# Queueing the scan's inverse blocks and the SSM's inputs behind the inverses' last stores

## The chip, the cores and the metric

The kernel runs on one core of one Trainium2 chip. A core has five engines that run side by side, each through its own list of instructions in a fixed order: TensorE (PE, with its weight loads shown as PEld), VectorE (DVE), ScalarE (ACT), GpSimd (POOL) and SyncE (SP). SP does no arithmetic here; it issues transfers (DMAs), one after the other. An instruction that waits for a semaphore holds up everything behind it on the same engine. A DMA is an issue on a queue (about half a microsecond of SP's time in this trace) and then the moving of the bytes by 16 shared DMA engines; its end is seen by others through a semaphore.

The metric is the device time of one launch in microseconds (us). Before the change it is 1614.11 us, the median of three runs (1608.63 to 1615.89).

## What is computed

One layer of a streaming encoder for 1024 prompt tokens and 32 sample tokens, 1056 columns in all. The layer is `x = LN(alpha*x + Mix(x))`, then `x = LN(alpha*x + MLP(x))`. Mix takes one input projection of x and feeds three groups: attention with a compressed KV latent (6 heads), an S5 state space model (the SSM, 16 groups with a 64-dimensional complex state) and RWKV-7 time mixing (6 heads of 64). Their outputs are joined and go through one output projection. The part of the reference around the change is the RWKV recurrence and the SSM's input:

```
def step(S, inp):                                   # RWKV, for each token
    r_t, w_t, k_t, v_t, kk_t, a_t = inp
    sa = einsum('bhij,bhj->bhi', S, -kk_t)
    S = S * w_t + sa[..., None] * (kk_t * a_t) + v_t[..., None] * k_t
    return S, einsum('bhij,bhj->bhi', S, r_t)

bu = einsum('gpc,btgc->btgp', b_bar, u_blk)         # SSM: inputs into states,
                                                    # then a scan over time and a readout
```

## The kernel before, in words

Stages. The input projection and all that is worked out per token for RWKV, attention and the SSM come first, up to about 300 us of the span. Then attention, RWKV and the SSM run interleaved, up to about 700 us. The output projection with the first layer norm follows, and from about 800 us on the MLP, where TensorE is almost always busy.

RWKV in chunks. The recurrence is done in chunks of 64 tokens as a triangular system. For each of the three pairs of heads (index p) and each chunk, a 64 x 64 unit-triangular matrix has to be inverted. `rwkv_inv` does it in two steps. First the 32 x 32 diagonal blocks are inverted on VectorE (31 steps on a tile `y`), and stored to DRAM: `zt_d` (transposed) and the fields 0 and 1 of `xt_d` (lines 765 and 766). Then they are loaded back in another layout as `zb` and `zc` (lines 777 and 778), and the off-diagonal block of each inverse is made by two rounds of small TensorE products (line 788), each followed by copies by VectorE out of PSUM (line 791). The second round's result, for p = 0, 1, 2, is stored to field 2 of `xt_d` at line 794: two DMAs for each p, six in all. The first four read `zb`, the last two `zc`. They are called the last stores below, S0, S1 and S2 by p.

The scan. `stage_rwkv` begins behind the inverses. It loads the two first blocks of operands `ld` (line 814), clears three tiles `xt` (POOL, line 1011), and fills them from `xt_d`: for each p six DMAs, four from the fields 0 and 1 (the diagonal blocks, lines 1015 and 1016) and two from field 2 (the off-diagonal block, line 1017), 18 in all. `xt` is read first in `rwkv_solve` (line 882). Ahead of that stands `rwkv_pairs`, which writes the tile `r` by DVE (line 835), ACT (line 841) and POOL (lines 853, 854). `r` and the SSM's tile `em` lie in memory that the inverses' tiles held before, so they wait for whatever read these tiles last: the last stores.

The SSM. `stage_s5` works in four quarters. Each loads `ut` from `u_d` (lines 619, 620), `em` (line 622), `ut`'s second part from `kt_d` by eight small DMAs (line 624) and `ces` from `tab_d` (line 628), multiplies `em` with `ut` on TensorE (line 633), loads `cl` over `em` (line 641), and goes on.

What sets the order. The kernel is written as generators: `stage_mix` yields the steps of attention with, from the 50th step on, a step of the SSM at every seventh; `stage_streams` yields the steps of the inverses and of the scan. `side_by_side` takes the steps of both in a fixed ratio. A planner at build time then orders each engine's instructions by dependencies, by its own estimate of the times and by priority: the order in which instructions were written, with the steps of `stage_streams` moved up by 120 places (`high_priority(PRIO)`). `issue_after(ins)` limits it: whatever is written inside the block on the engine of `ins` comes behind `ins` in that engine's list. It adds no semaphore. `side_by_side` uses it to keep TensorE's steps in the written order, and to hold SP's instructions of the second stream behind `g.sp_mark`, the last DMA of the first step of that stream (the load of `zc`, line 778). The SSM's steps are held behind `g.sp_mark` on SP too, and behind `g.scan_dve` on DVE. Where between the `zc` load and their consumers the 18 loads of `xt` and the SSM's loads stand in SP's list is left to the planner.

Of the kernel before, what the change touches and what calls it, by code (L numbers as in the profile page):

```python
# [406 lines left out]
def bc(ap, shape):  # L407
    return ap.broadcast_to(shape)
# [304 lines left out]
def hsl(i):  # L713
    return slice(64 * i, 64 * i + 64)
# [28 lines left out]
def rwkv_inv(g):  # L743


    nc = g.nc
    V = nc.vector
    H = 3 * NU
    nn = g.ip.tile([H, 2, 32, 32], F32, tag="nn", name="nn", bufs=1)
    yf = g.ip.tile([H, 2, 1024], F32, tag="y", name="y", bufs=1)  # L750
    y = yf.rearrange("v f (a b) -> v f a b", b=32)
    nc.gpsimd.memset(yf, 0.0)
    nc.gpsimd.memset(yf[:, :, 0:1024:33], 1.0)
    for p in range(3):
        (nc.sync if p % 2 else nc.scalar).dma_start(out=nn[NU * p:NU * p + NU], in_=g.mt_d[:, NU * p:NU * p + NU].rearrange("f v a b -> v f a b"))
    for s in range(31):
        m, n = s + 1, 31 - s
        tmp = g.ip.tile([H, 512], F32, tag="tmp", name="tmp", bufs=1)
        tv = tmp[:, :2 * m * n].rearrange("p (f m n) -> p f m n", f=2, n=n)
        V.tensor_tensor(out=tv, in0=bc(y[:, :, 0:m, s:s + 1], [H, 2, m, n]), in1=bc(nn[:, :, s:s + 1, s + 1:32], [H, 2, m, n]), op=ALU.mult)  # L760
        V.tensor_tensor(out=y[:, :, 0:m, s + 1:32], in0=y[:, :, 0:m, s + 1:32], in1=tv, op=ALU.add)
    yield
    zt = g.ip.tile([H, 32, 32], F32, tag="nn", name="zt", bufs=1)
    nc.scalar.activation(out=zt, in_=y[:, 0].rearrange("u i a -> u a i"), func=AF.Copy)
    nc.sync.dma_start(out=g.zt_d, in_=zt)
    nc.sync.dma_start(out=g.xt_d[:, 0:2], in_=y)

    zb = g.ip.tile([P, 2, 2, 16, 32], F32, tag="nn", name="zb", bufs=1)
    zc = g.ip.tile([P, 2, 16, 32], F32, tag="y", name="zc", bufs=1)
    parts = []  # L770
    for p in range(3):
        z, b = (zb[:, p, 0], zb[:, p, 1]) if p < 2 else (zc[:, 0], zc[:, 1])
        us = slice(NU * p, NU * p + NU)
        zs = g.zt_d[us].rearrange("(t c) a i -> c a t i", c=2)
        ys = g.xt_d[us].rearrange("(t c) f i j -> c f i t j", c=2)
        for c in range(2):
            nc.sync.dma_start(out=z[64 * c:64 * c + 32], in_=zs[c][:, 0:16])
            nc.sync.dma_start(out=z[64 * c + 32:64 * c + 64], in_=ys[c][1][:, 0:16])
        parts.append((z, b, ys))
    yield  # L780
    for o in (0, 32):
        for p, (z, b, ys) in enumerate(parts):
            l = b if o else g.n12[p]
            ps = g.pfs.tile([P, 16, 32], F32, tag="fs", name="pti")
            for t in range(16):
                for c in range(2):
                    rows = slice(64 * c + o, 64 * c + o + 32)
                    nc.tensor.matmul(out=ps[64 * c:64 * c + 32, t], lhsT=l[rows, t], rhs=z[rows, t], start=True, stop=True)
            for c in range(2):
                d = 64 * c + 32 - o  # L790
                V.tensor_copy(out=b[d:d + 32], in_=ps[64 * c:64 * c + 32])
            if o:
                for c in range(2):
                    nc.sync.dma_start(out=ys[c][2][:, 0:16], in_=b[64 * c:64 * c + 32])
            yield


# [8 lines left out]
def rwkv_load(g, t):  # L806

    nc = g.nc
    s, n = blk_tokens(t)
    ld = g.rp.tile([P, 3, 5, P], F32, tag="ld", name="ld", bufs=3)  # L810
    if n < P:
        nc.gpsimd.memset(ld, 0.0)
    for p in range(3):
        nc.sync.dma_start(out=ld[:, p, :, :n], in_=g.rw_d[p][:, 0:5, s:s + n])
    g.ld[t] = ld
# [45 lines left out]
def rwkv_nv(g, t):  # L861
    nc = g.nc
    r = g.r[t]
    pn = g.pr.tile([P, 3, 2, 64], F32, tag="pr", name="prn")
    for p in range(3):
        for h in range(2):
            for c in range(2):
                nc.tensor.matmul(out=pn[hsl(c), p, h], lhsT=r[hsl(c), p, K_N, h], rhs=r[hsl(c), p, K_V, h], start=True, stop=True)
    nc.scalar.activation(out=r[:, :, K_NV], in_=pn, func=AF.Copy)
# [106 lines left out]
def rwkv_norm(g, t):  # L976

    nc = g.nc
    s, n = blk_tokens(t)
    yc, sq = g.yc.pop(t)  # L980
    gate = g.rl.tile([P, 3, P], F32, tag="bg", name="gate", bufs=1)[:, :, :n]
    for p in range(3):
        nc.sync.dma_start(out=gate[:, p], in_=g.rw_d[p][:, 5, s:s + n])
    pv = g.pr.tile([P, 3, P], F32, tag="pr", name="prv")[:, :, :n]
    nc.tensor.matmul(out=pv, lhsT=g.bones, rhs=sq, start=True, stop=True)
    m = g.rl.tile([P, 3, P], F32, tag="m", name="m", bufs=1)[:, :, :n]
    nc.vector.tensor_scalar(out=m, in0=pv, scalar1=1.0 / 64, scalar2=GN_EPS, op0=ALU.mult, op1=ALU.add)
    iv = g.rl.tile([P, 3, P], F32, tag="iv", name="iv", bufs=1)[:, :, :n]
    rsqrt_newton(g, m, iv, sq)
    nc.vector.tensor_tensor(out=yc, in0=yc, in1=iv, op=ALU.mult)  # L990
    for p in range(3):
        nc.vector.tensor_scalar(out=yc[:, p], in0=yc[:, p], scalar1=g.vec[:, V_GNG + p:V_GNG + p + 1], scalar2=g.vec[:, V_GNB + p:V_GNB + p + 1], op0=ALU.mult, op1=ALU.add)
    nc.gpsimd.tensor_tensor(out=yc, in0=yc, in1=g.bn.pop(t), op=ALU.add)
    nc.gpsimd.tensor_tensor(out=yc, in0=yc, in1=gate, op=ALU.mult)
    s = TP if s == SOFF else s
    store(g, nc.gpsimd if t == ORDER[8] else None, g.mg_d[5:8, :, s:s + n].rearrange("k p t -> p k t"), yc)


def stage_rwkv(g):
    nc = g.nc  # L1000
    g.ld, g.r, g.wu, g.gq, g.xt, g.yb, g.yc, g.bn = {}, {}, {}, {}, {}, {}, {}, {}
    xts = [g.rp.tile([P, 9, 2, 64], F32, tag="xt", name="xt", bufs=3) for p in range(3)]
    for tag, n in (("wu", 1024), ("ut", NY * L5)):
        g.rp.tile([P, n], F32, tag=tag, name=tag, bufs=1)
    g.i2 = g.rp.tile([P, 64], F32, tag="i2", name="i2", bufs=1)
    nc.sync.dma_start(out=g.i2, in_=g.a["i2"])
    for t in ORDER[:2]:
        rwkv_load(g, t)
    for p in range(3):
        xt = xts[p]  # L1010
        nc.gpsimd.memset(xt, 0.0)
        src = g.xt_d[NU * p:NU * p + NU].rearrange("(t c) f i j -> c f i t j", c=2)
        for c in range(2):
            x = xt[hsl(c)].rearrange("p t h x -> p (t h) x")
            nc.sync.dma_start(out=x[0:32, :, 0:32], in_=src[c][0])
            nc.sync.dma_start(out=x[32:64, :, 32:64], in_=src[c][1])
            nc.sync.dma_start(out=x[0:32, 0:16, 32:64], in_=src[c][2][:, 0:16])
        g.xt[p] = xt

    for i in range(10):  # L1020
        t, u, v = (ORDER[j] if 0 <= j < 9 else None for j in (i, i - 1, i - 2))
        if i + 2 < 9:
            rwkv_load(g, ORDER[i + 2])
        if t is not None:
            yield from rwkv_pairs(g, t)
        if v is not None:
            rwkv_norm(g, v)
            yield
        if u is not None:
            g.yb[u] = g.rl.tile([P, 3, P], F32, tag="yb", name="yb", bufs=2)  # L1030
            yield from rwkv_ops(g, u)
        if t is not None:
            rwkv_nv(g, t)
            yield
            if u is not None:
                yield from rwkv_chain(g, u)
                rwkv_mean(g, u)
            rwkv_solve(g, t)
            yield
        if i == 8:  # L1040
            out_weights(g, WOUT[:3])
    out_weights(g, WOUT[3:])
# [251 lines left out]
def last_traced(g, engine):  # L1294

    return next(i for i in reversed(g.nc.cur_bb.bb.instructions) if i.engine == engine)
# [88 lines left out]
def out_weights(g, parts):  # L1385

    for k in parts:
        raw, hi, lo = g.wout_mem(k)
        load3(g, g.a["w_out"][:, k], raw, hi, lo)
        g.wout[k] = hi, lo  # L1390
# [118 lines left out]
def stage_mix(g):  # L1509

    with g.tc.tile_pool(name="pav", bufs=1, space=PSUM, reuse_waits="tile") as g.pav:
        ssm, n = stage_s5(g), 0
        for _ in stage_attn(g):
            yield
            n += 1
            if n > S5_FROM and n % S5_STEP == 0:
                with g.tc.issue_after(g.scan_dve), g.tc.issue_after(g.sp_mark):
                    next(ssm, None)
        for _ in ssm:
            yield  # L1520
# [354 lines left out]
```

## Time and profile before

| what | value |
|---|---|
| runs | 1614.11 us median (1608.63 to 1615.89) |
| profiled execution, its own time | 1613.95 us |
| its span, first to last instruction | 1612.2 us |
| mean granted TensorE clock | 0.964 |
| PE / PEld busy | 1488.8 / 1337.5 us (92% / 83%) |
| DVE / ACT / POOL busy | 920.5 / 510.7 / 416.5 us |
| DMA traffic | 123.50 MB in 112621 packets |

The times in the trace are microseconds from the span's first instruction. The rows of a timeline give the start, the duration, the engine, the line, the operation, the tiles and the count; the bracket behind a row gives how long the engine had been idle and which instruction or transfer ended the wait. Rows of SP are DMA issues, not the transfers themselves. In a table by stretches each engine has its busy time and, in brackets, its instructions, then the granted TensorE clock (1.00 is full), the mean busy share of the 16 DMA engines and GB/s.

### The profile page before, as it was taken

To read this page: it belongs to the slowest core of one execution; us is meant where nothing else is said; L and a number is where in the kernel's file an instruction comes from. 1 tells how busy PE (TensorE), PEld (TensorE's weight loads), DVE (VectorE), ACT (ScalarE), POOL (GpSimd) and SP (SyncE) were. 2 spreads that over 40 slices of the span, in tenths; PEclk is the share of its full clock that TensorE was granted. 3 is DMA by queue.
4 is the path that set the end of the run, shared out by engine and by line. 5 is a ranking of instruction groups with operands and counts; after the bars stand their busy time and mean duration, and the time that the engine had idled before them with its cause. 6 is when DMAs were issued, how large, how long until landed. Compare 5 with 4: busy or idle time off the path is not lost. (4 is left out here: it accounts for less than half of the span.)

```text
span 1612.2 us, 26346 instructions
## 1 busy us (share of the span) xinstructions
PE 1488.8 (92%) x10855; PEld 1337.5 (83%) x10855; DVE 920.5 (57%) x1676; ACT 510.7 (32%) x991; POOL 416.5 (26%) x394
## 2 busy tenths in 40 slices
PE   7899899587899888898999999999999999999995
PEld 7889786465667566566779999999999999999995
DVE  8466959363666544453865745454555454545458
ACT  4344433313544545542323111222111122221122
POOL 3713663520121101221412111222121112222123
PEclk9999999788999999999999999999999999999998
DMA  5314471372333221222612111111111111111012
GB/s 183 130 60 175 147 189 33 94 176 46 85 79 90 64 72 42 69 85 86 197 50 76 49 40 40 53 53 40 52 40 44 48 40 53 53 40 53 14 40 82
DMA packets 112621, 123.50 MB, mean 77 GB/s; under 512 B 51280, under 2 KB 87812, under 8 KB 112120
## 3 DMA queue, kind: packets, MB, share of 16 engines
q1 hardware_dynamic: 92516, 102.53, 21.9%
q10 hardware_dynamic: 19632, 18.27, 3.7%
q8 instruction: 85, 1.39, 0.4%
q0 software_dynamic: 352, 1.01, 0.2%
q14 instruction: 36, 0.29, 0.1%
HBM read 89.05 MB, written 32.68 MB: 76 GB/s over the span
## 5 line engine op out<-in xcount | busy, mean ns | idle before, releaser
L63 PE MATMUL acc<-xh,uphi 128*128 128x384 f32 (+1 forms) x768 | 248.9, 324 | 0.0
L65 PE MATMUL acc<-xl,uphi 128*128 128x384 f32 (+1 forms) x768 | 247.9, 323 | 0.0
L67 PE MATMUL acc<-xh,uplo 128*128 128x384 f32 (+1 forms) x768 | 247.6, 322 | 0.0
L1540 DVE TENSOR_TENSOR rl<-rl 128x384 f32<-128x384 f32 (+1 forms) x96 | 142.2, 1481 | 176.9 <-ACT rl L1539 175.3
L1568 DVE TENSOR_TENSOR yacc<-yacc,acc 128x384 f32<-128x384 f32 (+2 forms) x344 | 158.8, 507 | 111.7 <-PE acc L67 111.6
L63 PE MATMUL acc<-hh,dnhi 128*128 128x384 f32 (+2 forms) x736 | 209.2, 320 | 0.0
L65 PE MATMUL acc<-hl,dnhi 128*128 128x384 f32 (+2 forms) x736 | 207.1, 319 | 0.0
L67 PE MATMUL acc<-hh,dnlo 128*128 128x384 f32 (+2 forms) x736 | 197.4, 319 | 0.0
L50 POOL TENSOR_TENSOR dnlo<-dnraw,dnhi 128x1024 fp32r<-128x1024 f32 x30 | 72.5, 2418 | 337.7 <-ACT dnhi L49 322.4
L63 PEld LDWEIGHTS acc<-xh,uphi 128*128 128x128 f32 x768 | 144.1, 188 | 0.3 <-ACT xh L49 0.3
L65 PEld LDWEIGHTS acc<-xl,uphi 128*128 128x128 f32 x768 | 144.2, 188 | 0.0
L67 PEld LDWEIGHTS acc<-xh,uplo 128*128 128x128 f32 x768 | 144.2, 188 | 0.0
L50 POOL TENSOR_TENSOR uplo<-upraw,uphi 128x1024 fp32r<-128x1024 f32 x34 | 81.6, 2399 | 237.7 <-ACT uphi L49 237.7
L63 PE MATMUL acc<-xh,wmhi 128*128 128x384 f32 (+3 forms) x384 | 132.6, 345 | 9.3 <-ACT xh L49 8.4
L65 PE MATMUL acc<-xl,wmhi 128*128 128x384 f32 (+3 forms) x384 | 131.1, 341 | 1.6 <-DVE xl L50 1.6
L63 PEld LDWEIGHTS acc<-hh,dnhi 128*128 128x128 f32 x736 | 131.5, 188 | 0.0
L65 PEld LDWEIGHTS acc<-hl,dnhi 128*128 128x128 f32 x736 | 131.4, 188 | 0.0
L67 PE MATMUL acc<-xh,wmlo 128*128 128x384 f32 (+3 forms) x384 | 130.0, 339 | 0.0
L67 PEld LDWEIGHTS acc<-hh,dnlo 128*128 128x128 f32 x736 | 128.9, 188 | 0.0
L49 ACT ACTIVATE dnhi<-dnraw 128x1024 fp32r<-128x1024 f32 x30 | 31.8, 1060 | 299.8 <-PE acc L65 249.0
L1255 PE MATMUL av<-ptk,vo 128*128 128x512 f32 (+5 forms) x204 | 75.4, 453 | 22.3 <-POOL ptk L1282 19.2
L49 ACT ACTIVATE hh<-rl 128x384 fp32r<-128x384 f32 (+1 forms) x96 | 47.9, 499 | 148.9 <-DVE rl L1540 148.9
(489 smaller groups left out, 2880.5 us busy)
## 6 DMA issues: line engine op xcount, KB each, us to landing
upraw<-in_w_up SPq DMA_DIRECT2D x32, 512.0 KB
dnraw<-in_w_dn SPq DMA_DIRECT2D x30, 512.0 KB
ld<-rw SPq DMA_DIRECT2D x24, 320.0 KB
wmraw<-in_w_m SPq DMA_DIRECT2D x12, 512.0 KB
wo<-in_w_out SPq DMA_DIRECT2D x8, 512.0 KB
z<-in_xa SPq DMA_DIRECT2D x8, 512.0 KB
out_y<-o SPq DMA_DIRECT2D x8, 512.0 KB
xr<-in_xt SPq DMA_DIRECT2D x8, 384.0 KB
```

Source lines behind the costliest of these rows:

```text
L49: nc.scalar.activation(out=hi, in_=ps, func=AF.Copy)
L50: (lo_eng or nc.vector).tensor_tensor(out=lo, in0=ps, in1=hi.bitcast(F32), op=ALU.subtract)
L63: nc.tensor.matmul(out=outs[i], lhsT=lh, rhs=rhs[i][0], start=start, stop=False)
L65: nc.tensor.matmul(out=outs[i], lhsT=lh, rhs=rhs[i][1], start=False, stop=False)
L67: nc.tensor.matmul(out=outs[i], lhsT=ll, rhs=rhs[i][0], start=False, stop=stop)
L1255: nc.tensor.matmul(out=po[:, c:n], lhsT=vo[:w, kt].rearrange("p a x -> p (a x)")[:, 64 * i:64 * i + P], rhs=pt[:w, c:n], start=kt == tiles ...
L1540: nc.vector.tensor_tensor(out=r[:, :n], in0=r[:, :n], in1=r[:, :n], op=ALU.mult)
L1568: nc.vector.tensor_tensor(out=y, in0=y, in1=ps[i][:, :n], op=ALU.add)
```

## The change

Two limits on SP's list are changed. `rwkv_inv` now notes, after the last stores of each p, the last DMA written on SP as `g.inv_sp`; after p = 2 this is the second DMA of S2. The 18 loads of `xt` are written inside `issue_after(g.inv_sp)`, and the SSM's steps are held behind `g.inv_sp` instead of `g.sp_mark` on SP. No instruction is added or removed, no tile changes its size or place.

```
@@ rwkv_inv
             if o:
                 for c in range(2):
                     nc.sync.dma_start(out=ys[c][2][:, 0:16], in_=b[64 * c:64 * c + 32])
+                g.inv_sp = last_traced(g, mybir.EngineType.SP)
             yield
@@ stage_rwkv
-        for c in range(2):
-            x = xt[hsl(c)].rearrange("p t h x -> p (t h) x")
-            nc.sync.dma_start(out=x[0:32, :, 0:32], in_=src[c][0])
-            nc.sync.dma_start(out=x[32:64, :, 32:64], in_=src[c][1])
-            nc.sync.dma_start(out=x[0:32, 0:16, 32:64], in_=src[c][2][:, 0:16])
+        with g.tc.issue_after(g.inv_sp):
+            for c in range(2):
+                x = xt[hsl(c)].rearrange("p t h x -> p (t h) x")
+                nc.sync.dma_start(out=x[0:32, :, 0:32], in_=src[c][0])
+                nc.sync.dma_start(out=x[32:64, :, 32:64], in_=src[c][1])
+                nc.sync.dma_start(out=x[0:32, 0:16, 32:64], in_=src[c][2][:, 0:16])
         g.xt[p] = xt
@@ stage_mix
-                with g.tc.issue_after(g.scan_dve), g.tc.issue_after(g.sp_mark):
+                with g.tc.issue_after(g.scan_dve), g.tc.issue_after(g.inv_sp):
                     next(ssm, None)
```

## Prediction

> **What bounds the kernel now.** I read the busy shares of the page first, then a table by stretches, then the waits, and last the timelines of the engines around the inverses' last stores.
>
> ```profile
> PE 1488.8 (92%) x10855; PEld 1337.5 (83%) x10855; DVE 920.5 (57%) x1676; ACT 510.7 (32%) x991; POOL 416.5 (26%) x394
> ...
> 364.00:374.00 10.00, 0.12 (x2) 0.00 (x0) 2.30 (x5) 1.27 (x3) 2.87 (x5) 0.65 0.52 93
> 374.00:400.00 26.00, 25.73 (x247) 19.59 (x247) 10.65 (x28) 12.23 (x30) 0.65 (x5) 0.94 0.04 11
> 400.00:760.00 360.00, 322.31 (x3261) 239.61 (x3260) 189.67 (x413) 169.61 (x349) 54.26 (x111) 0.96 0.27 74
> ```
>
> TensorE (PE, first engine column) bounds the kernel as a whole. In the stretch from 364 to 374 us it does 0.12 us of work, while no other engine is busy for more than 2.87 us. Before and behind that hole it is close to full. The waits between 360 and 376 us name the cause:
>
> ```profile
> DVE r L835 <- DMA xt_d<-zc: 11.4, 1, 11.4
> POOL r L853 <- DMA xt_d<-zc: 10.7, 1, 10.7
> PE av L1255 <- POOL ptk L1282: 10.5, 2, 10.1
> ACT r L841 <- DMA xt_d<-zc: 7.7, 1, 7.7
> ```
>
> Three engines stop at the same transfer, the store of `zc` (S2), because `r` lies where `zc` lay. TensorE stops at `av`, which waits for a POOL memset that stands behind POOL's work on `r`. So the question is why S2 lands when it does. Here are VectorE's copies that make the data of the last stores, and then SP's list:
>
> ```profile
> 350.22 1.40 DVE L791 COPY zb<-pti 32x512 f32<-32x512 f32 x2 [1.25 <-PE pti L788]
> 355.75 1.40 DVE L791 COPY zb<-pti 32x512 f32<-32x512 f32 x2 [4.14 <-PE pti L788]
> ...
> 358.11 1.40 DVE L791 COPY zc<-pti 32x512 f32<-32x512 f32 x2 [0.23 <-PE pti L788]
> ```
>
> ```profile
> 338.59 0.52 SPq L619 DMA_DIRECT2D ut<-u_d x1
> 339.16 0.83 SPq L620 DMA_DIRECT2D ut<-u_d x1
> 340.03 0.84 SPq L628 DMA_DIRECT2D ces<-tab_d x1
> ...
> 347.61 1.68 SPq L814 DMA_DIRECT2D ld<-rw x3
> 349.39 0.46 SPq L1015 DMA_DIRECT2D xt<-xt_d x1
> ...
> 356.38 0.50 SPq L1016 DMA_DIRECT2D xt<-xt_d x1
> 356.97 3.97 SPq L624 DMA_DIRECT2D ut<-kt_d x5
> 361.04 1.07 SPq L794 DMA_DIRECT2D xt_d<-zb x2
> 362.16 0.54 SPq L624 DMA_DIRECT2D ut<-kt_d x1
> 363.08 0.86 SPq L1017 DMA_DIRECT2D xt<-xt_d x2
> 363.99 1.18 SPq L624 DMA_DIRECT2D ut<-kt_d x2
> 365.27 1.06 SPq L794 DMA_DIRECT2D xt_d<-zb x2
> 367.28 0.83 SPq L1017 DMA_DIRECT2D xt<-xt_d x2
> 368.22 0.96 SPq L794 DMA_DIRECT2D xt_d<-zc x2
> 370.28 0.84 SPq L1017 DMA_DIRECT2D xt<-xt_d x2
> 371.17 0.48 SPq L622 DMA_DIRECT2D em<-em_d x1
> ```
>
> The data of S0, S1 and S2 are ready at 351.62, 357.15 and 359.51 us (start plus duration of the copies). The stores go out at 361.04, 365.27 and 368.22: 9.4, 8.1 and 8.7 us later. In between SP is not waiting for data; it is issuing twelve loads of `xt` (349.39 to 356.88) and eight of `kt_d`, and between the stores it stands at line 1017 until the store before has landed. The queue, not the data, is what S2 waits for.
>
> **The change part by part.** No instruction is added; the edges carry no semaphore. Moved on SP are 16 of the 18 `xt` loads (only p = 2's two at line 1017 stood behind S2), `ut` x2, `ces` and the eight of `kt_d`. `em` stood behind S2 already. POOL's and ACT's queues carry none of them.
>
> *The stores.* SP gets to S0 no later than 349.29 (347.61 + 1.68) and then waits in turn for 351.62, 357.15 and 359.51. Whatever stands behind them on SP waits along, but that is now only the moved loads, `em`, and what stood behind `em` before. The second DMA of S2 is issued at about 359.51 and takes half of 0.96, so to 359.99. Before, S2 was issued by 369.18 (368.22 + 0.96) and `r` started at 370.88, 1.70 later. That gives 361.7 us in place of 370.9 for the first of these starts. POOL then has to go through its part, four operations on `r` and the memset behind them:
>
> ```profile
> 370.91 0.39 POOL L853 TENSOR_TENSOR r<-ld 128x96 f32<-128x96 f32 x1 [10.71 <-DMA xt_d<-zc]
> ...
> 373.97 0.23 POOL L1282 MEMSET ptk<- 64x64 f32 x2
> ```
>
> ```profile
> 363.85 0.27 PE L67 MATMUL st<-qh,kl 128*128 128x128 f32 x1
> 374.17 1.22 PE L1255 MATMUL av<-ptk,vo 128*128 128x256 f32 x2 [10.05 <-POOL ptk L1282]
> ...
> 383.13 1.53 PE L882 MATMUL prw<-r,xt 64*64 64x128 f32 x24
> ...
> 386.09 0.72 PE L633 MATMUL s5e<-ut,em 128*128 128x133 f32 x4
> ```
>
> From POOL's start to the memset are 3.06 us (370.91 to 373.97) and 0.20 more to `av`. From 361.75 on that ends at 365.0. TensorE is done with what stands ahead at 364.12, so the hole shrinks from 10.05 to 0.9 us: 9.1 us less. Bounds: 7.0, if the stores land more slowly by 2 us when the moved loads follow directly behind them; 10.05, the whole hole. I take 9.1.
>
> *The clock.* It had fallen when the hole ended:
>
> ```profile
> 348.00:352.00 4.00, 4.00 (x75) 3.82 (x75) 2.30 (x5) 0.00 (x0) 0.00 (x0) 0.50 0.76 112
> ...
> 374.00:378.00 4.00, 3.83 (x16) 3.28 (x17) 0.51 (x1) 0.79 (x2) 0.20 (x2) 0.59 0.00 0
> 378.00:383.00 5.00, 4.91 (x73) 4.09 (x71) 3.73 (x10) 3.20 (x8) 0.00 (x0) 1.00 0.02 3
> ```
>
> At a granted clock of 0.59 the 4 us from 374 to 378 hold work for 2.4 us at full clock, so up to 1.6 us go too if the clock stays up. The other end is nothing: in the first row the clock is at 0.50 without any idle time, with small matmuls at work. I take half, 0.8 us. The Trainium skill, page "TensorE: Matmul & The Clock Gate", section "HAM oscillation — how this bites in real kernels", says that the clock drops where TensorE idles for more than about 3.4 us. By that rule a hole of 0.9 us costs no clock and the sum is 1603.8; the row of 374 agrees, that of 348 does not follow from it.
>
> *The loads of `xt`, now late.* From 359.99 the twelve take 7.49 us (349.39 to 356.88) and the six of line 1017 0.86 + 0.83 + 0.84 = 2.53, together to 370.0; with 1.70 to land, 371.7. TensorE asks for them at line 882, at 383.13 - 9.1 = 374.0, or 372.4 with the whole clock. So they are covered with 0.7 to 2.3 us to spare: price 0. The cover is gone if the SSM's loads stand in front: `ut`, `ut`, `ces`, `em` and eight `kt_d` are 0.52 + 0.83 + 0.84 + 0.48 + 3.97 + 0.54 + 1.18 = 8.36 us of SP, the last `xt` lands at 380.1, and TensorE stands for 6.1 to 7.7 us.
>
> *The SSM's inputs, now late.* The first product of the SSM needs `ut` from `u_d` and `em`. TensorE asks at 386.09 - 9.9 = 376.2. Two rows of the waits tell how `em` lands (SP's own from 300 to 420, PE's from 400 to 560):
>
> ```profile
> SPq L641 <- DMA em<-em_d: 2.3, 1, 2.3
> ```
>
> ```profile
> PE s5e L633 <- DMA em<-em_d: 0.5, 1, 0.5
> ```
>
> If they follow `xt` in written order (`ut`, `ut`, `em`), `em` is issued by 371.8 and there 2.3 later, at 374.1: nothing. If `em` comes last, behind `kt_d` and `ces`, it is there at 380.7: 4.5 us of TensorE. The later quarter, whose loads are issued close ahead of their use, paid 0.5, the row nearest to this case; I take 0.5. `ces` and `kt_d` are used by VectorE and by products behind that, and have room.
>
> *What is late next.* `cl` waits for the SSM's product and moves up with it. From 400 us on TensorE idles 37.7 us of 360, in waits of at most 4.6 us whose releasers are engines that TensorE's own list feeds. So I carry the shift to the end in full. The sum: -9.1 - 0.8 + 0.5 = -9.4, against the profiled execution's 1613.95 (0.16 below the median shown): 1604.6 us.
>
> **The rivals.** *SSM loads ahead of `xt`.* The stores are early, but TensorE stops at line 882 for 6.9 us (the middle of 6.1 to 7.7) and the clock gains nothing: 1613.95 - 9.1 + 6.9 = 1611.8. For it: `ut` and `ces` went out at 338 to 341, before all `xt` loads. Against it: `stage_streams` has priority by 120 places, and in the rows above line 1017 goes out at 363.08 while two `kt_d` loads are still to come. 0.13.
>
> *The clock stays up.* TensorE goes through the 4 us behind the shortened hole at full clock and gains 1.6 instead of 0.8: 1603.8. For it speaks the row of 378 to 383, with 0.09 us idle and the clock at 1.00, against it the row of 348. 0.20. The page named above would have it so.
>
> *The hole is not the queue's doing.* If S2's place is taken by other work of SP (the planner moves the scan's later `ld` and `gate` loads up) or `r` waits for another tenant of that memory, the hole stays: about 1614. The rows speak against it, as every one of the three waits names `zc`'s store. 0.11.
>
> *Slower by the new plan.* The planner now believes that `xt` and the SSM's inputs come late, and may order ACT and POOL otherwise from there on; the place is `ptk`, which feeds `av`. Here are PE's waits from 400 to 760:
>
> ```profile
> PE av L1255 <- POOL ptk L1282: 8.7, 5, 4.6
> PE prb L846 <- ACT r L841: 3.9, 1, 3.9
> ```
>
> If `ptk` and `r` come late at twice as many places, both rows double: 12.6 us more, 1604.6 + 12.6 = 1617.2. It decides from 9.4 us on. For it: the hole itself came from such an order on POOL. Against it: TensorE's order is fixed by `issue_after`, and the other engines follow it. 0.13.
>
> **How the numbers follow.** The forecast has 0.43, with 1602 to 1608 as its own range (the stores' bounds of 7.0 and 10.05, `em` at 0 to 2). The range for 8 in 10 is 1600 to 1615: it takes in the clock, the first rival and most of the unchanged case; left out are what the new plan costs beyond 1615 and what it may gain beyond 1600. About 0.5% is what a measurement of this kernel can tell from no change: 8.1 us, a time under 1606.0 or over 1622.2. Of the forecast some seven tenths lie under 1606 (0.30), of the clock's case four fifths (0.16), and 0.05 come from plans that turn out better: 0.51 faster. Slower needs a plan worse by more than 17 us: 0.08. The rest, 0.41, is within.
>
> **What would show it.** Right: SP issues the six stores ahead of any `xt` load, S2 within a microsecond of the copy at line 791; the waits for `xt_d<-zc` shrink from 11.4 to about 2 us; TensorE's hole before `av` is about a microsecond; line 882 and the SSM's first product do not wait for `xt` or `em`; the clock from 365 to 369 tells the clock's share. Wrong: a wait of PE for `xt<-xt_d` or `em<-em_d` of several microseconds, S2 still issued behind other loads, or more than 38 us of idle TensorE between 400 us and 760 us less the shift.

## The result, and the profile after

The changed kernel takes 1600.72 us (median of 14 runs, 1597.66 to 1610.93) against 1612.07 us before (14 runs, 1608.63 to 1625.01). The ratio is 0.9933, 95% interval 0.9912 to 0.9954: 11 us or 0.67% less. Two later comparisons of the same two kernels gave 0.9941 (0.9921 to 0.9961) and 0.9942 (0.9919 to 0.9965). The profiled execution took 1603.22 us, with a span of 1601.4.

SP's list in the timeline of the changed kernel (its lines 1017 to 1019 are the 1015 to 1017 of before, and the line numbers of all that follows are two higher):

```profile
341.92 2.89 SPq L815 DMA_DIRECT2D ld<-rw  x3
348.10 6.62 SPq L794 DMA_DIRECT2D xt_d<-zb  x4
356.05 1.02 SPq L794 DMA_DIRECT2D xt_d<-zc  x2
357.17 0.44 SPq L1017 DMA_DIRECT2D xt<-xt_d  x1
...
366.29 1.15 SPq L1019 DMA_DIRECT2D xt<-xt_d  x1
367.48 0.49 SPq L619 DMA_DIRECT2D ut<-u_d  x1
368.01 0.51 SPq L620 DMA_DIRECT2D ut<-u_d  x1
368.57 0.51 SPq L622 DMA_DIRECT2D em<-em_d  x1
369.12 0.62 SPq L628 DMA_DIRECT2D ces<-tab_d  x1
370.74 6.04 SPq L624 DMA_DIRECT2D ut<-kt_d  x8
```

All six stores now stand ahead of any `xt` load. SP has nothing to issue between 344.8 and 348.1 us: it waits for data. Behind S2 come the 18 loads of `xt`, then the SSM's, in written order but for `ces`, which goes ahead of the eight `kt_d` loads. The copy that S2 waits for is this row of VectorE's timeline; the data are ready at 356.75, and SP is done with S2 at 357.07 (before: 359.51 and 369.18):

```profile
355.35 1.40 DVE L791 COPY zc<-pti 32x512 f32<-32x512 f32 x2 [0.23 <-PE pti L788]
```

What POOL and TensorE then do, from their timelines:

```profile
358.99 0.39 POOL L854 TENSOR_TENSOR r<-ld 128x96 f32<-128x96 f32 x1 [1.55 <-DMA xt<-xt_d]
...
361.73 0.23 POOL L1284 MEMSET ptk<- 64x64 f32 x2
```

```profile
361.09 0.28 PE L67 MATMUL st<-qh,kl 128*128 128x128 f32 x1
361.93 0.70 PE L1257 MATMUL av<-ptk,vo 128*128 128x256 f32 x2 [0.57 <-POOL ptk L1284]
...
369.44 1.53 PE L883 MATMUL prw<-r,xt 64*64 64x128 f32 x24
...
372.65 0.72 PE L633 MATMUL s5e<-ut,em 128*128 128x133 f32 x4 [0.18 <-DMA em<-em_d]
```

The hole of 10.05 us ahead of `av` is now 0.57. POOL's wait is short, 1.55 us; the row names a load of `xt`, but POOL does not wait for `xt`: the same wait is put down to `zc`'s store in the profile of e1, and in e7 below POOL starts on `r` at 360.20 us while the first `xt` load goes out at 364.13. The product with `xt` does not wait, that of the SSM waits 0.18 us. The stretch that was empty is full:

```profile
364.00:374.00 10.00, 9.73 (x138) 8.25 (x137) 5.87 (x13) 5.01 (x14) 0.00 (x0) 1.00 0.78 174
374.00:400.00 26.00, 23.35 (x264) 15.87 (x263) 11.95 (x25) 15.43 (x32) 3.37 (x12) 1.00 0.26 67
```

TensorE does 9.73 us of work in these 10, at a granted clock of 1.00. The orders of TensorE, VectorE, ScalarE and POOL are those of before; only SP's list has changed. So the start times of one and the same instruction of TensorE can be compared all along the two traces. The table has, for each run of this study, how much earlier it starts than in the profile of before (us), at six places that are named by their time before:

| run | 360 | 384 | 400 | 435 | 760 | 1600 |
|---|---|---|---|---|---|---|
| the change | 2.8 | 13.7 | 13.4 | 9.5 | 12.4 | 11.4 |
| e8, the change again | 4.2 | 15.1 | 15.1 | 14.8 | 15.8 | 15.6 |
| e10, the change again | 3.2 | 14.1 | 13.7 | 13.6 | 15.2 | 14.6 |
| e1, `xt` alone | 2.0 | 12.9 | 12.9 | 10.1 | 11.1 | 11.0 |
| e9, `xt` alone again | 5.3 | 12.4 | 12.4 | 11.2 | 15.2 | 14.9 |
| e2, SSM alone | 4.1 | 7.9 | 7.9 | 7.8 | 7.9 | 7.2 |
| e3, stores on POOL | 5.8 | 16.7 | 16.7 | 12.0 | 8.3 | 7.5 |
| e5, the same, Gelu held | 2.3 | 13.3 | 13.4 | 9.0 | 2.8 | 2.4 |
| e4, S2 delayed | 2.9 | 7.5 | 4.4 | 3.5 | -2.1 | -1.6 |
| e6, off-diagonal loads alone | 1.1 | 12.3 | 12.3 | 10.7 | 9.7 | 8.6 |
| e11, the same again | 4.1 | 15.1 | 15.1 | 14.9 | 16.6 | 16.0 |
| e7, `xt` delayed | 1.6 | 9.2 | 5.1 | 3.8 | 6.1 | 6.4 |

Two things are to be read from it. First, each run is already 1.1 to 5.8 us ahead at 360 us, where the change has done nothing yet. The stretch from 5 to 300 us of the two profiles, before and then the change, has the same order of work and another clock, 0.94 and 0.97:

```profile
5.00:300.00 295.00, 263.11 (x1623) 232.18 (x1624) 209.73 (x392) 121.15 (x216) 140.31 (x134) 0.94 0.41 130
```

```profile
5.00:300.00 295.00, 261.70 (x1639) 230.49 (x1640) 208.68 (x392) 121.79 (x217) 141.07 (x134) 0.97 0.41 131
```

Second, from 360 to 384 the change gains 10.9 us (13.7 - 2.8), and 10.9 again in e8 and e10. Whatever varies more than that is outside of this stretch: the change's profile loses 3.9 us between 400 and 435, e8 only 0.3. Here is that stretch in the profile of the change and in e8's:

```profile
400.00:408.00 8.00, 4.52 (x21) 2.68 (x23) 6.07 (x13) 4.11 (x9) 0.00 (x0) 0.83 0.02 3
408.00:415.00 7.00, 7.00 (x64) 6.08 (x62) 2.23 (x8) 1.63 (x5) 0.00 (x0) 0.71 0.07 16
```

```profile
400.00:408.00 8.00, 5.83 (x63) 4.08 (x63) 4.80 (x12) 5.38 (x12) 0.00 (x0) 1.00 0.08 16
408.00:415.00 7.00, 7.00 (x53) 5.51 (x46) 2.63 (x8) 2.84 (x6) 0.99 (x5) 1.00 0.08 17
```

It is one kernel, and TensorE is busy for all of the second row both times; the clock is 0.71 once and 1.00 the other time. In the change's profile it had fallen ahead of that row, at about 405.3 us, in the second of two waits of TensorE (the brackets):

```profile
403.19 1.10 PE L1121 MATMUL sck<-cpast,wkv 128*128 128x512 f32 x2 [2.24 <-DVE kl L50]
405.52 0.60 PE L1121 MATMUL sck<-ckv,wkv 128*128 128x32 f32 x2 [1.24 <-DVE kl L50]
```

It stays at 0.50 until about 412, over busy stretches too. The waits do not tell the clock by themselves: a wait of 2.49 us just before, at 396.42, cost the change's profile nothing, and the same wait in e8 was followed by 0.50 from 396 to 398 us. A profile by itself tells the total to no better than some 5 us here; the place of the change it tells to 0.1.

### The profile page after: what moved, and what is told of

Its sections match the earlier page's. It is cut to its first block, busy times and chain, and to the rows that moved or that the text cites. A ratio compares the mean times of both kernels' runs of the same rounds, so it can differ in the third digit from the quotient of the medians.

```text
span 1601.4 us, 26353 instructions
## 1 busy us (share of the span) xinstructions
PE 1483.2 (93%) x10855; PEld 1332.3 (83%) x10855; DVE 920.0 (57%) x1676; ACT 511.4 (32%) x991; POOL 416.3 (26%) x394
```

## The experiments

The theory is the prediction's: the last stores stood in SP's list behind loads, `r` waited for S2, and TensorE for `r`. The rivals are that the SSM's loads or the traffic of the early loads are what mattered, that the queue is not the point, and that the cover under the moved loads is larger or smaller than thought. Each run is compared with the kernel before on the same chip.

**e1 and e9: the `xt` loads alone.** The changed kernel with the SSM's steps held behind the old mark:

```
-                with g.tc.issue_after(g.scan_dve), g.tc.issue_after(g.inv_sp):
+                with g.tc.issue_after(g.scan_dve), g.tc.issue_after(g.sp_mark):
```

> One part alone: the 18 loads of xt behind the inverses' last stores, the SSM's loads held behind the old mark as before. SP's list then has ut, ut, ces early, the eight kt_d loads ahead of S0, and xt behind S2. Theory (S2 was late because SP was issuing the xt loads): SP reaches S0 at about 349.3 + 5.5 = 354.8 by the times of before, so only S0 is later than its data; S2 goes out with its data, r starts 9 us sooner, and the time is 10 to 11 us below before, like the whole change. Rival (the SSM's loads, 0.8 MB of them at 338 to 341 us where the DMA engines are full, are what delayed things): less than half of that, 0 to 5 us.

Measured: 1600.85 us, ratio 0.9903 (0.9875 to 0.9931). From 360 to 384 it gains 10.9 us, like the whole change. (e9, a second execution of this kernel, is told below; its profile gains 7.1 there.) SP's list, from e1's timeline:

```profile
347.56 5.38 SPq L624 DMA_DIRECT2D ut<-kt_d  x8
353.04 2.44 SPq L794 DMA_DIRECT2D xt_d<-zb  x4
356.81 1.25 SPq L794 DMA_DIRECT2D xt_d<-zc  x2
```

Only S0 is late; S2 goes out with its data (VectorE's copy ends at 357.51). So the 18 `xt` loads carry the gain, and the SSM's eight early loads of `kt_d` do no harm as long as TensorE is not faster.

**e2: the SSM's loads alone.** The changed kernel with the `xt` loads free again:

```
-        with g.tc.issue_after(g.inv_sp):
+        if True:
             for c in range(2):
```

> The other part alone: the SSM's loads behind the last stores, the xt loads free as before. SP's list has twelve xt loads, then S0, its two loads of line 1017, S1, two, S2. Theory: the twelve loads end at 347.1 + 7.5 = 354.6, S0 lands at about 357.4, the two loads of line 1017 follow, S1 goes out at about 358.2 and lands at about 361, S2 goes out at about 361.8 and lands at 364.5 by the times of before; that is 6.4 us sooner than before and 2.8 later than the whole change. Time 6 to 8 us below before; the hole of TensorE is 3 to 4 us. Rival (the SSM's part does the work): as much as the whole change, 10 to 11 us, with a hole of about 1 us.

Measured: 1610.89 us, ratio 0.9974 (0.9951 to 0.9998). 4 us, less than the 6 to 8 expected, and far from the rival. From 360 to 384 it gains 3.8. SP's list and the hole, from e2's timeline, and two stretches of e2 around it:

```profile
352.48 0.97 SPq L794 DMA_DIRECT2D xt_d<-zb  x2
356.09 0.84 SPq L1019 DMA_DIRECT2D xt<-xt_d  x2
357.01 0.97 SPq L794 DMA_DIRECT2D xt_d<-zb  x2
359.06 0.84 SPq L1019 DMA_DIRECT2D xt<-xt_d  x2
359.95 1.01 SPq L794 DMA_DIRECT2D xt_d<-zc  x2
...
366.16 1.22 PE L1257 MATMUL av<-ptk,vo 128*128 128x256 f32 x2 [6.13 <-POOL ptk L1284]
```

```profile
362.00:366.00 4.00, 0.00 (x0) 0.00 (x0) 2.48 (x5) 1.27 (x3) 2.88 (x5) 0.58 0.84 167
366.00:370.00 4.00, 3.84 (x15) 3.26 (x16) 0.45 (x1) 0.77 (x2) 0.19 (x2) 0.57 0.13 34
```

The loads of line 1019 stand between the stores. Each waits until the store before has landed, and the next store waits with it: S1 ends at 357.98 and the next load is issued at 359.06; S0 ends at 353.45 and its loads go out at 356.09. S2 leaves at 359.95, though its data are ready at 355.42. The hole is 6.13 us, and the clock stays at 0.57 behind it, so nothing of the clock's share is gained either. The expectation took the landing right (S2 at 361.8 by the times of before) but not that TensorE itself ran ahead in this execution, so that the same late S2 makes a larger hole. Whether it did so in the eleven other runs, which have no profile, is not known.

**e3 and e5: the stores on another queue.** The kernel before with the six stores on POOL's queue; e5 also holds the SSM's Gelu behind ScalarE's last instruction written before it:

```
-                    nc.sync.dma_start(out=ys[c][2][:, 0:16], in_=b[64 * c:64 * c + 32])
+                    nc.gpsimd.dma_start(out=ys[c][2][:, 0:16], in_=b[64 * c:64 * c + 32])
 e5 also:
+    with g.tc.issue_after(last_traced(g, mybir.EngineType.Activation)):
         log_exp_table(g, [nc.scalar.activation(out=zt, in_=zt, func=AF.Gelu_apprx_tanh)], False)
```

> The kernel before with one edit: the six last stores are issued on POOL's queue instead of SP's; every load keeps its old place. Theory (the stores stood in a queue behind loads): S2 goes out with its data at 359.5 and, with the 2.6 us that POOL's DMAs take to land in the page of before, r starts at about 362.3; the hole is about 1.5 us, the time 8 to 10.5 us below before. Rival (what matters is that the loads come late, because they compete with the stores for the DMA engines or the memory): the loads are as early as ever, so the hole stays above 5 us and the gain under 4 us.

Measured: 1611.71 us, ratio 0.9975 (0.9954 to 0.9997). The total speaks for the rival, the trace does not: the hole is closed to 0.6 us and the gain from 360 to 384 is 10.9, with every load as early as before. Much of it is lost again later: the lead falls by 4.6 us from 384 to 435, where the change's own profile loses 4.2, and by another 5.0 from 560 to 600 us (10.3 to 5.3). These are ScalarE's timeline and TensorE's waits around it in e3:

```profile
575.47 1.28 ACT L683 ACT_TABLE_LOAD   x1 [9.14 <-DMA zt<-z_d]
```

```profile
PE av L1255 <- ACT po L1260: 9.9, 1, 9.9
```

The new plan puts the Gelu six instructions further forward on ScalarE, ahead of the evictions that feed `av`, and both engines stand until its loads have landed. (The kernel before waits 3.9 us in that stretch too, at another place, so the net loss is 5.0 and not 9.9.) It is the prediction's rival of a worse plan, in another kernel than the one forecast.

> As e3 (the kernel before with the last stores on POOL's queue), with one more edit: the SSM's Gelu is held behind ACT's last instruction written before it, because in the plan of e3 it stood six instructions earlier on ACT than in the kernel before and ACT waited 9.1 us there for its input, TensorE 9.9 us with it. Theory: e3's small gain is the closed hole less this new wait; with the Gelu back where ACT does not stop ahead of ptk, the gain is 8 to 11 us against before. Rival (the stores' queue alone is worth only what e3 showed): 3 to 5 us again.

Measured: 1606.70 us, ratio 0.9945 (0.9924 to 0.9967), by the ratio 8.9 us less than before. The gain from 360 to 384 is 11.0. So the stores alone, taken off SP's list, are worth in that stretch what the theory says, and the traffic of the early loads is not the cause. That the Gelu's place made up the difference in the totals is less certain: the intervals of e3 and e5 overlap, and the profiled execution of e5, the slowest of its eight, loses nearly all of its gain behind 384 us, 7 of the 11 us between 600 and 760; the cause of that is open.

**e4: S2 delayed.** The changed kernel with 16 loads of 4 KB each, into a tile that nothing reads, between S1 and S2. S2's own two DMAs are put inside `issue_after(g.inv_sp)` as well, so that they stand behind these loads; of the edit only the loads are shown:

```
+                if p == 1:
+                    pad = g.ap0.tile([P, P], F32, tag="pad", name="pad")
+                    for k in range(16):
+                        with g.tc.issue_after(g.inv_sp):
+                            nc.sync.dma_start(out=pad[:, 8 * k:8 * k + 8], in_=g.a["ident"][:, 8 * k:8 * k + 8])
+                        g.inv_sp = last_traced(g, mybir.EngineType.SP)
```

> The changed kernel with 16 small loads (into a tile that nobody reads) issued on SP between S1 and S2. At 0.35 to 0.45 us each they hold SP for 5.6 to 7.2 us from 354.7 on, so S2 goes out at about 361 instead of 356 in the times of the changed kernel. Theory (TensorE's hole follows S2 one to one): the hole comes back at 4 to 6 us and the time is 4 to 7 us above the changed kernel, 4 to 7 us below before. Rival (something else ends the hole now, and S2 has room): the time of the changed kernel.

Measured: 1616.70 us, ratio 1.0004 (0.9983 to 1.0024). All of the gain is gone, more than expected. From e4's timelines, SP first and then TensorE:

```profile
354.67 8.59 SPq L801 DMA_DIRECT2D pad<-in_ident  x16
363.35 0.91 SPq L795 DMA_DIRECT2D xt_d<-zc  x2
```

```profile
366.69 1.09 PE L849 MATMUL prt<-ident,ld 128*128 128x128 f32 x4 [4.96 <-DVE r L844]
...
380.34 0.72 PE L633 MATMUL s5e<-ut,em 128*128 128x133 f32 x4 [1.28 <-DMA em<-em_d]
```

A load takes SP 0.54 us (8.59 / 16), not 0.35 to 0.45, and S2 goes out 6.7 us behind its data (ready at 356.64). The hole is back with 4.96 us, the SSM's product waits 1.28 for `em`, and the clock's share is lost (0.50 from 364 to 370): at 400 us the lead over 360 is 1.5 instead of 10.6. The hole has moved, though. This plan has two memsets of `ptk` on POOL ahead of `r`, which the kernels before and after the change have behind it:

```profile
360.36 0.15 POOL L1292 MEMSET ptk<- 64x64 f32 x1 [3.02 <-ACT ptk L1290]
361.62 0.15 POOL L1292 MEMSET ptk<- 64x64 f32 x1 [1.11 <-ACT ptk L1290]
```

So TensorE gets through `av` and stops at `prt`, which waits for VectorE's part of `r`. The theory's direction is shown: a late S2 makes `r` late, and TensorE stands. Its one to one is not: the late S2 takes `xt`, `em` and the clock along, and the plan is not quite the same. It also suggests that the memset moved alone would not have closed the hole. Behind 435 us e4 loses another 5.6. One wait there, of a product of the scan for VectorE, is 4.1 us; VectorE's order differs a little in this plan, and why it comes was not followed further.

**e6 and e11: only the off-diagonal blocks' loads behind the stores.** The changed kernel with the edge around the third load alone:

```
-        with g.tc.issue_after(g.inv_sp):
+        if True:
             ...
-                nc.sync.dma_start(out=x[0:32, 0:16, 32:64], in_=src[c][2][:, 0:16])
+                with g.tc.issue_after(g.inv_sp):
+                    nc.sync.dma_start(out=x[0:32, 0:16, 32:64], in_=src[c][2][:, 0:16])
```

> The changed kernel with only six of the 18 xt loads, those of the off-diagonal blocks, behind the last stores; the twelve diagonal loads are free again, and SP has them ahead of S0 as in e2. The SSM's loads stay behind. Theory (in e2 the stores were late because SP stood between them at loads that wait for the store before to land, not because of the twelve loads): S0 goes out at about 352.5, S1 and S2 with their data, the hole is about 0.6 us, and the time is that of the changed kernel, 9 to 13 us below before. Rival (the twelve diagonal loads must come late): the time of e2, 3 to 5 us below before, with a hole of several us.

Measured: 1602.20 us, ratio 0.9914 (0.9894 to 0.9933). From e6's timeline:

```profile
351.99 4.38 SPq L794 DMA_DIRECT2D xt_d<-zb  x4
357.69 1.02 SPq L794 DMA_DIRECT2D xt_d<-zc  x2
358.81 3.11 SPq L1020 DMA_DIRECT2D xt<-xt_d  x6
...
363.30 0.70 PE L1258 MATMUL av<-ptk,vo 128*128 128x256 f32 x2 [0.30 <-POOL ptk L1285]
```

With twelve `xt` loads ahead of S0 as in e2, but no load that waits between the stores, the hole is 0.30 us and the gain from 360 to 384 is 11.2. So in e2 it was the waiting loads between the stores that made S2 late. (These six held back alone, with the SSM's loads free, were not run.)

**e7: `xt` and the SSM's inputs delayed.** The changed kernel with 12 of the same small loads behind S2, ahead of `xt`:

```
+                if p == 2:
+                    pad = g.ap0.tile([P, P], F32, tag="pad", name="pad")
+                    for k in range(12):
+                        with g.tc.issue_after(g.inv_sp):
+                            nc.sync.dma_start(out=pad[:, 8 * k:8 * k + 8], in_=g.a["ident"][:, 8 * k:8 * k + 8])
+                        g.inv_sp = last_traced(g, mybir.EngineType.SP)
```

> The changed kernel with 12 of the small loads of e4 placed on SP behind S2 and ahead of the xt loads, 0.54 us each as measured there, 6.4 us together. r is as early as in the changed kernel; only xt and the SSM's inputs are later. By the trace of the changed kernel TensorE reaches the product with xt just as xt lands (369.4 us), so theory: it waits there for 5 to 7 us, and the time is 5 to 8 us above the changed kernel, 3 to 6 us below before. Rival (the loads have the 0.7 to 2.3 us to spare that the prediction worked out, and the next waits take up some of the rest): 1 to 4 us above the changed kernel.

Measured: 1611.39 us, ratio 0.9979 (0.9965 to 0.9993), 6 to 7 us above the changed kernel of the same chip (e8, 1604.45 and 0.9941). From e7's timelines of SP and TensorE:

```profile
358.33 5.70 SPq L800 DMA_DIRECT2D pad<-in_ident  x12
...
374.21 0.50 SPq L1025 DMA_DIRECT2D xt<-xt_d  x1
...
376.41 1.11 PE L889 MATMUL prw<-r,xt 64*64 64x128 f32 x6 [1.10 <-DMA xt<-xt_d]
```

The hole ahead of `av` stays closed (0.58 us). TensorE waits at the product with `xt`, four times and 3.7 us in all, as the loads land one after the other; the last is issued by 374.71 and used at 376.41, 1.70 us later. The lead falls by 7.3 us from 380 to 400 (10.9 less 3.5 over 360). The waits are 3.7 of it, and the clock is nearly all of the rest:

```profile
376.00:380.00 4.00, 3.59 (x37) 2.89 (x37) 0.24 (x1) 0.57 (x2) 0.00 (x0) 0.50 0.90 232
380.00:384.00 4.00, 4.00 (x18) 3.33 (x17) 1.58 (x4) 1.82 (x5) 0.00 (x0) 0.69 0.27 75
```

These 8 us hold 4.8 us at full clock, 3.2 less. So the theory has the total (5 to 8) but not the wait (5 to 7). In the changed kernel the same 1.70 behind the last `xt` load (366.29 + 1.15) gives 369.14, and TensorE begins the product at 369.44: the cover is 0.3 us there. It is larger where the last load is needed: e7's last wait stands ahead of the last 6 of the 24 products, which with an even share of the 1.53 us come 1.1 us later, so the cover is about 1.4 us by this estimate. e1 bears that out: its last `xt` load is issued by 369.18, and the product begins at 370.26, only 1.08 later, and has no wait.

**e8, e10: the change again, and e9, e11 beside e10.**

> The changed kernel once more beside the others of this call, for their comparison on one chip: 9 to 13 us below before. In its profile the shift against the profile of before is looked at ahead of 300 us, where the order of all engines is the same in both: whatever is there is the chip's clock in that execution and not the change.

> The changed kernel as the measure for the other two of this call: 9 to 13 us below before.

> The kernel of e1 (only the xt loads behind the last stores) beside the whole change and e6's kernel on one chip. Theory: the SSM's part of the change adds nothing, because with the xt loads away SP reaches S0 in time either way; the three times lie within 3 us of each other. Rival: e1's ratio of 0.9903 against the change's 0.9933 was real, and the SSM's part costs 3 to 5 us (its first product then waits for em).

> The kernel of e6 (only the six loads of the off-diagonal blocks and the SSM's loads behind the last stores). Theory: it closes the same hole, and its xt and em land some 4 us earlier, which is worth at most the 0.2 us that TensorE waited for em in the changed kernel: no difference to the change. Rival: the earlier xt and em also spare later waits, and it beats the change by 2 us or more.

Measured: the change 1604.45 us (0.9941, 0.9921 to 0.9961) in e8 and 1603.84 us (0.9942, 0.9919 to 0.9965) in e10; `xt` alone 1600.30 us (0.9917, 0.9899 to 0.9935); the off-diagonal loads and the SSM's 1600.12 us (0.9915, 0.9895 to 0.9934). Over all runs the means are 1603.7 (31 runs of the change), 1600.8 (12) and 1601.2 (12). Both smaller edits are never behind the whole change, and by the means 2.5 to 3 us ahead, two to three standard errors. So the expectations of no difference are not borne out, and the rival of 2 us or more is the likelier one; beside each other (e9 to e11) the medians are 3.5 and 3.7 us apart, but the intervals overlap. The profiles show no cause of that size: the waits for `em` are 0.2 us in the change, 0.4 in e10 and none in e8 or in the other two kernels, what the profiles gain or lose behind 384 us (the table) has no side, and e9 has a larger hole of its own. TensorE's clock in e9, in two stretches:

```profile
358.00:361.00 3.00, 0.82 (x5) 0.49 (x3) 2.31 (x5) 1.31 (x3) 2.43 (x4) 1.00 0.82 130
361.00:364.00 3.00, 2.33 (x8) 1.95 (x9) 0.00 (x0) 0.21 (x1) 0.64 (x3) 0.57 0.83 133
```

In that execution the small products ahead of the stores ran at full clock, TensorE came 2.9 us earlier, and SP, held up by the eight `kt_d` loads, did not: the hole was 2.85 us and cost the clock behind it. So `xt` alone leaves SP late where TensorE is fast, and the whole change does not; why it is not slower for that is left open.

## Why the prediction was right, by its own steps

*What bounds.* The stores left in time once SP was free, and all else followed. Shown by e1, e5 and e6, which free the stores in three ways and gain 10.9, 11.0 and 11.2 us in the same stretch, by e9, where S2 goes out 1.5 us behind its data, the hole is 2.85 and the gain 7.1, and by e4, which delays S2 and loses it.

*The stores.* Forecast 9.1 us; TensorE gained 9.5 at `av` (12.24 at `av`, less 2.76 at 360), for the hole left is 0.57 and not 0.9. The lower bound, stores that land 2 us more slowly with the loads directly behind them, did not come: POOL starts on `r` 1.92 us behind S2's issue (358.99 less 357.07), against 1.73 before (370.91 less 369.18).

*The clock.* Forecast 0.8, half of 1.6; measured 1.4 (13.69 at 384, less 12.24), the clock at 1.00 through the whole stretch. The term was sized too small; its half was a choice between two ends. The rule of the Trainium skill ("TensorE: Matmul & The Clock Gate", section "HAM oscillation — how this bites in real kernels"), that idle times over about 3.4 us drop the clock, came out right for the holes of 0.3 to 0.6 us, which kept it, and for those of 6.13 in e2 and 4.96 in e4, which lost it. As a threshold it did not hold: 2.85 us were enough in e9, the clock is at 0.50 in e7 behind waits of at most 1.26, and the change's profile loses it in the wait of 1.24 shown above, behind one of 2.24. The row of 348, which the prediction read as a low clock without idle time, is the middle of such a stretch: in the profile before the clock is at 1.00 until 346, at 0.76 from 346 to 347 and at 0.50 until 353, and TensorE had idled 1.2 us between 343 and 345. Whether that or the small products did it is not shown.

*`xt`.* Forecast as covered, with 0.7 to 2.3 us to spare; the landing of 1.70 us is what e7 shows, and the cover is 0.3 at the start of the product, less than was said, and about 1.4 (estimated) at the products that need the last load. The prediction took the start for the time of need. The price without cover is e7's: 6 to 7 us.

*The SSM's inputs.* Forecast 0.5 us, measured 0.2, nothing and 0.4 in the three profiles of the change. `em` needed longer than the 2.3 us that were taken: issued by 369.08, used at 372.65, 3.57 later. It had 3.4 us until TensorE asked, and not the 4.4 that the prediction left it.

*The sum.* -9.4 forecast. In the stretch the profile has -9.5, -1.4 and +0.2, together -10.7, and the timed ratios stand for 9.4 to 10.8 us. The carry to the end, taken in full, holds within what single executions add or take: the table's last column less its first is 8.6, 11.4 and 11.4 for the three profiles of the change. (Over the 360 us from 387 on TensorE idles 38.3 us in the change's profile, against 37.7 from 400 before; 38 was named as a sign of being wrong, and the lead falls by 1.0 there.) The 1600.72 us lie under the forecast's own 1602 to 1608, and just inside the wide range. The gain, 9.4 to 10.8 us by the ratios, is at most 1.4 over the sum; the rest of the distance is the kernel before, which ran at 1612.07 beside the change and not at the 1613.95 that the forecast starts from.

*The rivals.* The SSM's loads did not go ahead of `xt`; the order was that of writing and priority. The hole was the queue's doing. The worse plan did not come with this change, since no other engine's order moved; in e3 it came, with a wait of 9.9 us at one place and a net loss of 5.0. The rival in which the clock stays up is the one that happened, and its 1603.8 is nearer to the result than the forecast's 1604.6. The share of the clock is 1.4 to 1.5 in all three profiles of the change.

## What to carry to other kernels

Look in the list of the issuing queue for stores behind loads: if a store's source is memory that later work takes over, the store's place in the queue sets when that work starts, whatever the data's own time is. Loads that wait for a store to land belong behind the last store, not between two stores. And when an edit's total disappoints, follow one engine's equal instructions through both traces: the gain may be there, and given back where the plan put something else.

## What the runs showed of the hardware

The granted clock of TensorE varies between executions of one kernel at places with the same work (0.71 and 1.00 between 408 and 415 us above), and once it has fallen it stays low for some microseconds of full work (from 405.3 to 412 there). A wait of 2.49 us was followed by 0.50 in one execution and not in another; 2.85 us were followed by it in e9. The stretch from 5 to 300 us has 0.94 before and 0.97 in the change, and the leads at 360 us, ahead of what the change does, are between 1.1 and 5.8 us. A DMA costs SP about 0.5 us of its list whether it is small or not: 0.54 on average for the 4 KB loads of e4 and 0.48 in e7, 0.43 to 0.51 for the 72 KB loads of `xt` in the change.
